# Post norms split by column halves, one factor pass moved by one unit, and score matmuls of two head groups interleaved, in a one-core decoder layer

## The chip, the cores and the metric

The kernel runs on one core of a Trainium2 chip. The metric is the device time of one execution in microseconds (us), lower is better. One profiled execution of the kernel gives the durations that are used below; three timed executions give the median that the change is compared with.

The engines are named as in the profile: PE is the matrix engine (its loading of the stationary operand is PEld), DVE the vector engine, ACT the scalar engine, POOL the GpSimd engine, and SP the engine whose queue issues nearly all DMAs here. [...]

## The reference

One layer is applied to a prompt of 1024 tokens and to 64 sample tokens (8 sequences of 8), all of width 1024, in float32. Post norms stand on the outputs, pre norms on the inputs:

```python
x = x + 0.5 * rms_norm(swiglu(rms_norm(x, norm_ffn1_pre), ffn1_w_gu, ffn1_w_down), norm_ffn1_post)
h = rms_norm(x, norm_mix_pre)
z = h @ w_in + b_in                      # q, k, v, hq, hf, hi, hg
a = attend(q, k, v, sinks)               # 8 heads of 64, 2 kv heads, window 128, sinks
o = hgrn2(silu(hq), f, hi, state)        # 4 heads of 128 x 128, gated recurrence
x = x + rms_norm(concat(rms_norm(a), rms_norm(o) * silu(hg)) @ w_out, norm_mix_post)
x = x + 0.5 * rms_norm(swiglu(rms_norm(x, norm_ffn2_pre), ffn2_w_gu, ffn2_w_down), norm_ffn2_post)

def rms_norm(x, g):
    return x * rsqrt(mean(x * x, axis=-1) + EPS) * g
```

The hidden width of each FFN is 2816. Outputs are both token groups, the last keys and values, and the recurrent states.

## The kernel before

**Token groups.** The 1088 tokens are cut into group 0 (two prompt blocks of 128 and the 64 samples, 320 columns) and groups 1 and 2 (three prompt blocks of 128 each). Group 0 is kept with features on the partitions all the way. Groups 1 and 2 come out of the down projections and out of `w_out` with tokens on the partitions, as two halves of 512 columns, `y[0]` and `y[1]`, each of shape 128 x 3 x 512: `y[hf][:, i]` is a piece of 128 tokens by 512 columns.

**Precision.** A weight or activation is split into a high and a low part (`split`, `load_w`, lines 251 to 263: a cast on ACT at L252 and a subtraction on DVE at L253), and every product is three matmuls (`mm3`, L273, L274, L275).

**FFN for groups 1 and 2.** The two groups are multiplied together by a seven-product scheme of the Strassen kind. In `f.up`, unit u (of 22) forms weight combinations on DVE (`factor`, `comb` at L662), seven products on PE, and evicts them (`evict`). After two units `left(u)` forms on POOL the combinations of the activations and stores them to DRAM (`FA`). The combinations of the down weights are formed in the same stage: `right_load(u)` loads four row pieces (L740), and `right_form(u)` computes four differences on POOL (L746 to L750) and stores them to DRAM (`FB`). Both are called in even units, at product 1 and at product 7. The down projections of groups 1 and 2 are then run product by product in `pair(ms)`: PA = (1, 6, 2), PB = (5, 3), PC = (7, 4). After PA, `y[0]` of group 1 is complete; after PB, `y[1]` of group 1; after product 7, `y[1]` of group 2; after product 4, `y[0]` of group 2 (`put`, L896 to L914).

**Streams.** Side work is written as generators. `stream(name, gen, rate)` registers one, `tick()` advances each by its rate after a piece of PE's main work, and `need(name)` emits what is left of it. The streams here: `m0`, `m1`, `m2` are the mixers (attention and recurrence) of the groups; `c0`, `c1`, `c2` are the norms between two stages for each group. The rate constants are `RA1` for the norms after FFN 1 and `RB1` for those after the mixer. The program order made this way is then re-ordered per engine by a scheduler that works on a simulated timeline, so that the place of an instruction in its queue is fixed at build time.

**Post norm of groups 1 and 2.** `post_n` (L411) loads both halves of the gain row, broadcast to 128 partitions (`bcast_row`, L396, scaled at L398), takes six sums of squares on ACT (`row_rms`, L388), the inverse root on DVE (L389, L390 and `rsqrt`), and then for each of six pieces (`post_block`) loads the residual piece `xt` (L405), multiplies by root and gain (L407, DVE), adds the residual (L408: half 0 on POOL, half 1 on DVE), and stores the result (L409). It is followed in the stream by the pre norm of the next stage: `pre_n` (before `w_in`) or `pre_s` (before FFN 2, with its own squares at L388, scaling at L435/L437 or L468/L470, and PE transposes at L445 or L488). `need("c1")` stands ahead of `w_in_units(1)`, and `need("c2")` ahead of `w_in_units(2)` and of FFN 2's `f2.up`.

**Output projection.** `w_out_units(n, ys)` for groups 1 and 2 runs, for each half, four weight pieces into three PSUM banks (of four of tag `mm`) and evicts them with three ACT copies (L1442).

**Attention.** `attn_block(n, b)` handles one block of 128 queries and 8 heads. It loops over the two kv groups g. For each g it makes two PSUM banks (`pr`), each with the scores of two heads (L1096). The heads of g = 0 lie on partitions 0 to 63 of the operands, those of g = 1 on partitions 64 to 127, so each score matmul contracts over 64 partitions. Then follow the masked row maximum on DVE (L1101), exponentials on ACT (L1110), transposes (L1121) and the products with v (L1134). The recurrence's steps are the PE matmuls at L1165 and L1189, which wait for DVE (L1200) and POOL (L1202).

## Time and profile before

| | |
|---|---|
| median of 3 timed executions | 2056.77 us (2053.96 to 2057.99) |
| the profiled execution's own time | 2056.1 us |
| its span, first to last instruction | 2054.4 us |
| mean granted PE clock | 0.989 |
| PE busy | 2017.0 us (98%) |
| DVE busy | 1453.1 us (71%) |
| ACT busy | 930.8 us (45%) |
| POOL busy | 572.4 us (28%) |

The profiled execution lies 1.7 us above its span and 0.7 us below the median. Read the table as follows: PE is the engine that is nearly always at work, so time can be saved in two ways only, by less time of PE's own work or by fewer stretches in which PE waits or runs at a lower granted clock. The other engines matter where PE waits for them.

| stage (PE) | about, us from the span's start |
|---|---|
| FFN 1: up and down, product set PA | 0 to 660 |
| w_in of group 0 | 660 to 735 |
| PB and PC, with the mixer of group 0 beside them | 735 to 870 |
| w_in and w_out stages, FFN 2's first units for group 0 | 870 to 1470 |
| FFN 2: up | 1470 to 1805 |
| FFN 2: down, all product sets | 1805 to 2046 |

### The profile page before, as it was taken

The numbers are of one execution on the slowest core, as the hardware profiler recorded it, in microseconds if no ns is written. First come the engines' busy times: TensorE is split into PE (matmuls) and PEld (weight loads), VectorE is DVE, ScalarE is ACT, GpSimd is POOL, SyncE is SP. The second block draws the span as 40 slices with busy tenths as digits, with TensorE's granted clock in tenths as the row PEclk, the third lists the DMA queues.
The fourth block names the chain that finished last, engine by engine and source line by source line (L and its number), as shares of the span: only waits on it lengthen the run. The fifth ranks groups of instructions, "written<-read, shape, count | busy, mean of one in ns | idle before, by whom it ended". The sixth has DMA issues, their size and how long they took to land.

```text
span 2054.4 us, 34787 instructions
## 1 busy us (share of the span) xinstructions
PE 2017.0 (98%) x13337; PEld 1884.0 (92%) x13337; DVE 1453.1 (71%) x2414; ACT 930.8 (45%) x1661; POOL 572.4 (28%) x523
## 2 busy tenths in 40 slices
PE   9999999999999999899999999899999999999998
PEld 8999999999988988798899898798899999999886
DVE  6775657886568556876668755775888888755657
ACT  6544333444454345344344433655544444444453
POOL 0033334554114001312212301311145555410202
PEclk9999999999999999899999999999999999999999
DMA  8545345556777546555344343535665556576874
GB/s 254 158 157 167 119 162 187 189 181 205 239 236 211 154 144 185 151 161 163 109 104 133 91 133 94 160 102 168 197 209 188 175 194 208 181 239 220 291 253 140
DMA packets 371976, 360.09 MB, mean 175 GB/s; under 512 B 40195, under 2 KB 293970, under 8 KB 371794
## 3 DMA queue, kind: packets, MB, share of 16 engines
q1 hardware_dynamic: 371009, 356.42, 55.3%
q8 instruction: 105, 1.72, 0.4%
q10 hardware_dynamic: 800, 1.44, 0.2%
q14 instruction: 62, 0.50, 0.1%
HBM read 279.85 MB, written 78.94 MB: 175 GB/s over the span
## 4 chain that ended last, share of the span: by engine, by line
PE 90%; DVE 5%; DMA 2%; issue 1%; ACT 1%; SPq 0%; POOL 0%; DVEq 0%; ACTq 0%
PE mm L273 26%; PE mm L274 26%; PE mm L275 26%; PE pv L1134 1%; PE sc L1096 1%; PE c L273 1%; PE c L275 1%; PE c L274 1%; DMA raw<-in_ffn_w_gu_dram 1%; PE lv L1165 1%; DVE wspl L253 1%; DVE w L253 1%; PE pT L1121 1%; DVE big L407 1%; DVE t L662 1%
## 5 line engine op out<-in xcount | busy, mean ns | idle before, releaser
L273 PE MATMUL mm<-h,wsph 128*128 128x320 f32 (+1 forms) x1296 | 411.7, 321 | 6.9 <-ACT sg L623 4.5
L274 PE MATMUL mm<-h,wsph 128*128 128x320 f32 (+1 forms) x1296 | 412.8, 319 | 0.0
L275 PE MATMUL mm<-h,wspl 128*128 128x320 f32 (+1 forms) x1296 | 410.6, 318 | 1.2 <-DVE sm L321 1.0
L253 DVE TENSOR_TENSOR wspl<-raw,wsph 128x1024 fp32r<-128x1024 f32 x202 | 257.8, 1278 | 125.6 <-ACT wsph L252 125.2
L252 ACT CAST wsph<-raw 128x1024 fp32r<-128x1024 f32 x202 | 211.2, 1048 | 293.1 <-PE mm L274 221.3
L253 DVE TENSOR_TENSOR w<-raw,w 128x512 fp32r<-128x512 f32 (+1 forms) x226 | 233.6, 1036 | 93.3 <-ACT w L252 89.4
L252 ACT CAST w<-raw 128x512 fp32r<-128x512 f32 (+1 forms) x226 | 169.7, 754 | 220.1 <-PE mm L274 110.1
L273 PEld LDWEIGHTS mm<-h,wsph 128*128 128x128 f32 x1296 | 245.0, 190 | 10.4 <-ACT sg L623 5.2
L274 PEld LDWEIGHTS mm<-h,wsph 128*128 128x128 f32 x1296 | 245.5, 189 | 3.4 <-issue 2.7
L275 PEld LDWEIGHTS mm<-h,wspl 128*128 128x128 f32 x1296 | 245.1, 189 | 2.8 <-DVE sm L321 1.2
L273 PE MATMUL mm<-h,w 128*128 128x384 f32 x704 | 236.6, 336 | 0.4 <-DVE big L716 0.4
L274 PE MATMUL mm<-h,w 128*128 128x384 f32 x704 | 236.3, 336 | 0.0
L275 PE MATMUL mm<-h,w 128*128 128x384 f32 x704 | 231.1, 336 | 0.7 <-DVE w L253 0.7
L700 POOL TENSOR_TENSOR big<-big 128x384 f32<-128x384 f32 x88 | 106.3, 1208 | 318.8 <-ACT big L713 235.0
L253 DVE TENSOR_TENSOR w<-t,w 128x512 fp32r<-128x512 f32 x176 | 177.7, 1019 | 21.5 <-ACT w L252 21.5
L274 PE MATMUL mm<-w,h 128*128 128x512 f32 x462 | 181.2, 392 | 0.0
L273 PE MATMUL mm<-big,w 128*128 128x384 f32 x528 | 176.6, 334 | 4.1 <-ACT w L252 4.1
L275 PE MATMUL mm<-w,h 128*128 128x512 f32 x462 | 180.1, 392 | 0.0
L273 PE MATMUL mm<-w,h 128*128 128x512 f32 x462 | 179.3, 392 | 0.0
L274 PE MATMUL mm<-big,w 128*128 128x384 f32 x528 | 176.5, 334 | 0.0
L275 PE MATMUL mm<-big,w 128*128 128x384 f32 x528 | 176.2, 334 | 0.0
L273 PEld LDWEIGHTS mm<-h,w 128*128 128x128 f32 x704 | 132.6, 188 | 1.1 <-DVE big L716 0.8
(344 smaller groups left out, 3929.7 us busy)
## 6 DMA issues: line engine op xcount, KB each, us to landing
raw<-in_ffn_w_gu_dram SPq DMA_DIRECT2D x156, 512.0 KB
raw<-in_ffn_w_down_dram SPq DMA_DIRECT2D x74, 512.0 KB
raw<-in_w_in_dram SPq DMA_DIRECT2D x54, 512.0 KB
ar<-fa SPq DMA_DIRECT2D x70, 384.0 KB
big<-in_ffn_w_down_dram SPq DMA_DIRECT2D x88, 256.0 KB
fb<-big SPq DMA_DIRECT2D x44, 512.0 KB
raw<-fb SPq DMA_DIRECT2D x40, 512.0 KB
fa<-big SPq DMA_DIRECT2D x22, 768.0 KB
```

The lines of the kernel that those rows point to most:

```text
L252: S.copy(hi, src)
L253: (lo_eng or V).tensor_tensor(lo, src, hi.bitcast(F32), op=ALU.subtract)
L273: PE.matmul(out, a[0], b[0], start=first, stop=False, skip_group_check=resume)
L274: PE.matmul(out, a[0], b[1], start=False, stop=False, skip_group_check=resume)
L275: PE.matmul(out, a[1], b[0], start=False, stop=last, skip_group_check=resume)
L407: V.scalar_tensor_tensor(t, t, r, gb[hf], op0=ALU.mult, op1=ALU.mult)
L662: V.tensor_tensor(t, x, y, op=ALU.subtract)
L700: G.tensor_tensor(e[:, i], e[:, i], e[:, i + 1], op=ALU.mult)
L1096: PE.matmul(bank[:, i * 256:i * 256 + wk], zq[64 * g:64 * g + 64, 2 * pr + i, b * P:(b + 1) * P], kx[64 * g:64 * g + 64, k0:k0 + wk], star ...
L1121: PE.transpose(bank[:, (i * nk + kb) * P:(i * nk + kb + 1) * P], pt[pr][:, i, kb * P:(kb + 1) * P], ident)
L1134: PE.matmul(ob[:, hd * 64:hd * 64 + 64], pT[pr][:, (i * nk + kb) * P:(i * nk + kb + 1) * P], vn[:, vb, g * 64:g * 64 + 64], start=kb == 0, ...
L1165: PE.matmul(b4[cs, a, :32], x[:, a, cs], y[:, a, cs], start=True, stop=True)
```

## The change

There are five edits.

1. **Post norms by halves.** `bcast_row` becomes `gain_row` for one half. The new `half_n` takes the three squares of one half on ACT and multiplies its three pieces by the gain row on DVE; for FFN 1 it is started for a half as soon as that half is complete (`half1`). `post_n` then adds the sums, takes the root, and handles each piece with one DVE instruction: piece times root plus `xt`. All adds on POOL in `post_n` are gone.
2. **Mixer's post norm at eviction.** In `w_out_units` the ACT copy of each bank is replaced by an ACT square of the bank (with its sum) and a DVE multiplication of the bank by the gain row into `y`. The gain row is loaded per half, between the half's matmuls and its eviction.
3. **Order of the stages after PB.** PC = (7, 4) is run as two calls, (7,) and (4,), and the half of group 2 that product 7 completes is normed beside product 4. `RA1` goes from 0.6 to 0.75.
4. **Down factors in odd units.** `right_load` and `right_form` are called in odd units, for the same weight rows.
5. **Alternating score matmuls.** `attn_block` loops over `pr` outside and over g inside: the four score matmuls of a step go to two banks, one for each g, and alternate between partitions 0 to 63 and 64 to 127. The small per-head vectors are indexed accordingly.

```diff
-    def bcast_row(ap, scale):
...
+    def gain_row(ap, scale, hf):
+        g = tmp2("gb")
+        nc.sync.dma_start(g, ap[0:1, hf * 512:hf * 512 + 512].partition_broadcast(P))
+        if scale is not None:
+            V.tensor_scalar(g, g, scale, None, op0=ALU.mult)
         return g
...
-            V.scalar_tensor_tensor(t, t, r, gb[hf], op0=ALU.mult, op1=ALU.mult)
-            (V if hf else G).tensor_tensor(t, t, xt, op=ALU.add)
...
+    def half_n(y, hf, sm, gpost, scale):
+        for i in range(3):
+            S.activation(junk, y[hf][:, i], AF.Square, accum_out=sm[:, 0, 4 * hf + i:4 * hf + i + 1])
+        g = gain_row(gpost, scale, hf)
         yield
         for i in range(3):
+            V.tensor_tensor(y[hf][:, i], y[hf][:, i], g, op=ALU.mult)
+            yield
+
+    def post_n(n, y, sm, xsrc, xdst):
+        V.tensor_tensor(sm[:, 0, 0:3], sm[:, 0, 0:3], sm[:, 0, 4:7], op=ALU.add)
+        V.tensor_scalar(sm[:, 0, 0:3], sm[:, 0, 0:3], 1.0 / D, EPS, op0=ALU.mult, op1=ALU.add)
+        rsqrt(sm[:, 1, 0:3], sm[:, 0, 0:3], (sm[:, 2, 0:3], sm[:, 3, 0:3]))
+        for i in range(3):
+            for hf in range(2):
+                cs = slice(hf * 512, hf * 512 + 512)
+                xt = tmp2("xt")
+                nc.sync.dma_start(xt, xsrc[i * P:(i + 1) * P, cs])
+                t = y[hf][:, i]
+                V.scalar_tensor_tensor(t, t, sm[:, 1, i:i + 1], xt, op0=ALU.mult, op1=ALU.add)
+                nc.sync.dma_start(xdst[i * P:(i + 1) * P, cs], t)
             yield
...
         def right_load(u):
-            k = f.units[u][0]
+            k = f.units[u - 1][0]
...
-                    if m == 1 and u % 2 == 0:
+                    if m == 1 and u % 2:
                         right_load(u)
                     product(u, m)
                     evict(u, m)
-                    if m == 7 and u % 2 == 0:
+                    if m == 7 and u % 2:
                         right_form(u)
...
+            for pr in range(2):
+                pt, banks = [], [axbank("sc") for _ in range(2)]
+                for i in range(2):
+                    for g in range(2):
+                        PE.matmul(banks[g][:, i * 256:i * 256 + wk],
+                                  zq[64 * g:64 * g + 64, 2 * pr + i, b * P:(b + 1) * P],
+                                  kx[64 * g:64 * g + 64, k0:k0 + wk], start=True, stop=True)
...
+                g = gain_row(A["norm_mix_post"], None, hf)
                 for i in range(3):
-                    S.copy(y[hf][:, i], banks[i])
+                    S.activation(junk, banks[i], AF.Square, accum_out=sm[:, 0, 4 * hf + i:4 * hf + i + 1])
+                    V.tensor_tensor(y[hf][:, i], banks[i], g, op=ALU.mult)
...
-    RA0, RA1, RB0, RB1 = 1.2, 0.6, 0.6, 0.8
+    RA0, RA1, RB0, RB1 = 1.2, 0.75, 0.6, 0.8
...
-        f1.pair(PB, False, last=lambda: f1.begin_pair(PC, False))
+        half1(1)
+        f1.pair(PB, False, last=lambda: f1.begin_pair((7,), False))
         done1(1)
-        f1.pair(PC, False)
+        f1.pair((7,), False, last=lambda: f1.begin_pair((4,), False))
+        half1(2)
+        f1.pair((4,), False)
         done1(2)
...
-        stream("c1", post_n(1, f2.ys[1], x2N[0], A["norm_ffn2_post"], 0.5, O[0][0, t0:t0 + 384]), 1.5)
+        y, sm = f2.ys[1], small()
+        stream("c1", seq(*[half_n(y, hf, sm, A["norm_ffn2_post"], 0.5) for hf in range(2)],
+                         post_n(1, y, sm, x2N[0], O[0][0, t0:t0 + 384])), 1.5)
```

More of the change, by code (lines that the diff above doesn't have):

```diff
@@ L391, in row_rms @@
         rsqrt(sm[:, 1, b0:b1], sm[:, 0, b0:b1], (sm[:, 2, b0:b1], sm[:, 3, b0:b1]))
-    def bcast_row(ap, scale):
-        g = [tmp2("gb"), tmp2("gb")]
-        for hf in range(2):
-            nc.sync.dma_start(g[hf], ap[0:1, hf * 512:hf * 512 + 512].partition_broadcast(P))
-            if scale is not None:
-                V.tensor_scalar(g[hf], g[hf], scale, None, op0=ALU.mult)
-        return g
-    def post_block(n, y, i, r, gb, xsrc, xdst):
-        for hf in range(2):
-            cs = slice(hf * 512, hf * 512 + 512)
-            xt = tmp2("xt")
-            nc.sync.dma_start(xt, xsrc[i * P:(i + 1) * P, cs])
-            t = y[hf][:, i]
-            V.scalar_tensor_tensor(t, t, r, gb[hf], op0=ALU.mult, op1=ALU.mult)
-            (V if hf else G).tensor_tensor(t, t, xt, op=ALU.add)
-            nc.sync.dma_start(xdst[i * P:(i + 1) * P, cs], t)
@@ L411, in post_n @@
-    def post_n(n, y, xsrc, gpost, scale, xdst):
-        gb = bcast_row(gpost, scale)
-        sm = small()
-        row_rms(n, y, [0, 1, 2], sm)
+    def gain_row(ap, scale, hf):
[3 more added lines that the diff above has]
+            V.tensor_scalar(g, g, scale, None, op0=ALU.mult)
+        return g
+    def half_n(y, hf, sm, gpost, scale):
+        for i in range(3):
+            S.activation(junk, y[hf][:, i], AF.Square, accum_out=sm[:, 0, 4 * hf + i:4 * hf + i + 1])
+        g = gain_row(gpost, scale, hf)
@@ L416, in post_n @@
         yield
         for i in range(3):
-            post_block(n, y, i, sm[:, 1, i:i + 1], gb, xsrc, xdst)
+            V.tensor_tensor(y[hf][:, i], y[hf][:, i], g, op=ALU.mult)
[12 more added lines that the diff above has]
+                nc.sync.dma_start(xdst[i * P:(i + 1) * P, cs], t)
@@ L743, in right_form @@
         def right_form(u):
-            k = f.units[u][0]
+            k = f.units[u - 1][0]
             a, b = downs.pop(u)
@@ L1085, in attn_block, with of @@
             sm, mx = small(), small()
-            pts = {}
             ob = None
-            for g in range(2):
-                hs = slice(4 * g, 4 * g + 4)
-                pt = []
-                for pr in range(2):
-                    bank = axbank("sc")
+            def of(x, pr):
+                return x.rearrange("p (g r i) -> p g r i", g=2, r=2)[:, :, pr]
+            for pr in range(2):
[5 more added lines that the diff above has]
+                                  kx[64 * g:64 * g + 64, k0:k0 + wk], start=True, stop=True)
+                for g in range(2):
                     p = t2((P, 2, 256))
@@ L1095, in attn_block @@
                     for i in range(2):
-                        PE.matmul(bank[:, i * 256:i * 256 + wk],
-                                  zq[64 * g:64 * g + 64, 2 * pr + i, b * P:(b + 1) * P],
-                                  kx[64 * g:64 * g + 64, k0:k0 + wk], start=True, stop=True)
+                        hd = 4 * g + 2 * pr + i
+                        V.tensor_tensor_reduce(out=p[:, i, :wk], in0=banks[g][:, i * 256:i * 256 + wk], in1=mask,
+                                               op0=ALU.add, op1=ALU.max, scale=1.0, scalar=NEG,
+                                               accum_out=mx[:, 0, hd:hd + 1])
+                V.scalar_tensor_tensor(of(sm[:, 0], pr), of(mx[:, 0], pr), 0.125, of(sinkb, pr),
+                                       op0=ALU.mult, op1=ALU.max)
+                V.tensor_scalar(of(sm[:, 1], pr), of(sm[:, 0], pr), -1.0, None, op0=ALU.mult)
+                for g in range(2):
                     for i in range(2):
                         hd = 4 * g + 2 * pr + i
-                        V.tensor_tensor_reduce(out=p[:, i, :wk], in0=bank[:, i * 256:i * 256 + wk], in1=mask,
-                                               op0=ALU.add, op1=ALU.max, scale=1.0, scalar=NEG,
-                                               accum_out=mx[:, 0, hd:hd + 1])
-                V.scalar_tensor_tensor(sm[:, 0, hs], mx[:, 0, hs], 0.125, sinkb[:, hs],
-                                       op0=ALU.mult, op1=ALU.max)
-                V.tensor_scalar(sm[:, 1, hs], sm[:, 0, hs], -1.0, None, op0=ALU.mult)
-                for pr in range(2):
-                    for i in range(2):
-                        hd = 4 * g + 2 * pr + i
-                        S.activation(pt[pr][:, i, :wk], pt[pr][:, i, :wk], AF.Exp, bias=sm[:, 1, hd:hd + 1],
+                        S.activation(pt[g][:, i, :wk], pt[g][:, i, :wk], AF.Exp, bias=sm[:, 1, hd:hd + 1],
                                      scale=0.125, accum_out=mx[:, 1, hd:hd + 1])
-                V.tensor_tensor(sm[:, 2, hs], sinkb[:, hs], sm[:, 0, hs], op=ALU.subtract)
-                S.activation(sm[:, 2, hs], sm[:, 2, hs], AF.Exp)
+                V.tensor_tensor(of(sm[:, 2], pr), of(sinkb, pr), of(sm[:, 0], pr), op=ALU.subtract)
+                S.activation(of(sm[:, 2], pr), of(sm[:, 2], pr), AF.Exp)
                 yield
@@ L1116, in attn_block @@
                 pT = []
-                for pr in range(2):
+                for g in range(2):
                     bank = axbank("pT")
@@ L1121, in attn_block @@
                             PE.transpose(bank[:, (i * nk + kb) * P:(i * nk + kb + 1) * P],
-                                         pt[pr][:, i, kb * P:(kb + 1) * P], ident)
+                                         pt[g][:, i, kb * P:(kb + 1) * P], ident)
                     t = t2()
@@ L1128, in attn_block @@
                     ob = axbank("pv")
-                for pr in range(2):
+                for g in range(2):
                     for i in range(2):
@@ L1134, in attn_block @@
                             PE.matmul(ob[:, hd * 64:hd * 64 + 64],
-                                      pT[pr][:, (i * nk + kb) * P:(i * nk + kb + 1) * P],
+                                      pT[g][:, (i * nk + kb) * P:(i * nk + kb + 1) * P],
                                       vn[:, vb, g * 64:g * 64 + 64], start=kb == 0, stop=kb == nk - 1)
@@ L1416, in mixer, with w_out_units @@
                 nc.sync.dma_start(O[4][0, 0].rearrange("h k v -> k h v"), state[0])
-        def w_out_units(n, ys):
+        def w_out_units(n, ys, sums):
             w = WIDTH[n]
@@ L1431, in w_out_units @@
             y = ys[n] = [big(F32, (P, 3, 512)), big(F32, (P, 3, 512))]
+            sm = sums[n] = small()
             for hf in range(2):
@@ L1475, in misc @@
                               A[src][0, :, 8:128].rearrange("b w g d -> b w (g d)"))
+    sums = {}
     def done1(n):
@@ L1481, in done1, with half1 @@
         else:
-            stream(f"c{n}", seq(post_n(n, y, xN[n - 1], A["norm_ffn1_post"], 0.5, x1N[n - 1]),
-                                pre_n(n, y, g, hmix)), RA1)
+            need("half")
+            stream(f"c{n}", seq(half_n(y, 2 - n, sums[n], A["norm_ffn1_post"], 0.5),
+                                post_n(n, y, sums[n], xN[n - 1], x1N[n - 1]), pre_n(n, y, g, hmix)), RA1)
+    def half1(n):
+        sums[n] = small()
+        stream("half", half_n(f1.ys[n], n - 1, sums[n], A["norm_ffn1_post"], 0.5), RA1)
     with tc.tile_pool(name="f1", bufs=1) as tp:
@@ L1508, in done_mix @@
         else:
-            stream(f"c{n}", seq(post_n(n, y, x1N[n - 1], A["norm_mix_post"], None, x2N[n - 1]),
+            stream(f"c{n}", seq(post_n(n, y, sums[n], x1N[n - 1], x2N[n - 1]),
                                 pre_s(n, y, g, part, f2.SF)), RB1)
@@ L1524, in tile_step @@
         stream("m1", mixer(1), RM[1])
-        w_out_units(0, ym)
+        w_out_units(0, ym, sums)
         done_mix(0)
@@ L1532, in tile_step @@
         stream("m2", mixer(2), RM[2])
-        w_out_units(1, ym)
+        w_out_units(1, ym, sums)
         done_mix(1)
@@ L1537, in tile_step @@
         need("m2")
-        w_out_units(2, ym)
+        w_out_units(2, ym, sums)
         done_mix(2)
@@ L1559, in ready_half @@
         y = f2.ys[2][1]
-        gb = tail["gb"] = bcast_row(A["norm_ffn2_post"], 0.5)
+        gb = tail["gb"] = [gain_row(A["norm_ffn2_post"], 0.5, hf) for hf in range(2)]
         sm = tail["sm"] = small()
```

## Prediction

> **What bounds the kernel now.** I read the page's busy shares first, then its line of granted PE clock. PE works nearly all the time:

> ```profile
> span 2054.4 us, 34787 instructions
> PE 2017.0 (98%) x13337; PEld 1884.0 (92%) x13337; DVE 1453.1 (71%) x2414; ACT 930.8 (45%) x1661; POOL 572.4 (28%) x523
> ...
> PEclk9999999999999999899999999999999999999999
> ```

> So two things can save time: less PE work, or fewer waits of PE. The timeline of PE, which gives in brackets the idle time before a row and its releaser, puts the waits of the middle stages in three places (two rows of each of the first two):

> ```profile
> 852.77 0.66 PE L1165 MATMUL lv<-t,t 128*32 128x32 f32 x32 [3.43 <-DVE t L1200]
> 862.03 1.09 PE L1071 MATMUL oT<-ident,t 128*128 128x128 f32 x4 [2.09 <-DVE t L1067]
> ...
> 1288.66 0.47 PE L273 MATMUL mm<-h,wsph 128*128 128x320 f32 x1 [2.34 <-ACT sg L623]
> 1306.00 0.66 PE L1165 MATMUL lv<-t,t 128*32 128x32 f32 x32 [3.25 <-DVE t L1200]
> ```

> With their smaller neighbours, place B (838 to 863) has 7.8 us of idle PE, place C (1283 to 1310) 7.3, and place D (1430 to 1513, FFN 2's first units) 6.6, of which 4.1 is one wait at 1481.79. After them the granted clock falls. Windows of 10 us (length, then busy us of PE, PEld, DVE, ACT, POOL, then clock, DMA share, GB/s) show that, and that DVE is full beforehand:

> ```profile
> 840.00:850.00 10.00, 7.96 (x97) 5.78 (x95) 9.09 (x36) 7.82 (x22) 3.02 (x3) 1.00 0.98 272
> 850.00:860.00 10.00, 6.18 (x72) 5.71 (x72) 7.67 (x18) 3.88 (x9) 2.69 (x6) 0.60 0.67 149
> 860.00:870.00 10.00, 7.97 (x44) 7.56 (x45) 7.57 (x18) 3.52 (x7) 0.62 (x1) 0.72 0.19 52
> ...
> 1475.00:1485.00 10.00, 6.79 (x43) 6.47 (x41) 10.00 (x10) 1.62 (x3) 7.88 (x4) 1.00 0.40 149
> ```

> PE's busy time times the missing share of clock is 6.18 x 0.40 + 7.97 x 0.28 = 4.7 us at B; in the same way 3.9 at C (0.83 and 0.66) and 1.5 at D (0.83). So B, C and D cost 21.7 of idle and 10.1 of slow clock, 31.8 us. DVE is full there with post norms, as DVE's timeline of group 2's mixer norm shows; POOL's rows lie beside it:

> ```profile
> 1426.88 6.16 DVE L407 SCALAR_TENSOR_TENSOR big<-big,sm,gb 128x512 f32<-128x512 f32 x6
> 1432.97 1.78 DVE L408 TENSOR_TENSOR big<-big,xt 128x512 f32<-128x512 f32 x1
> ...
> 1439.09 0.68 DVE L408 TENSOR_TENSOR big<-big,xt 128x512 f32<-128x512 f32 x1
> ```
> ```profile
> 1427.72 1.74 POOL L408 TENSOR_TENSOR big<-big,xt 128x512 f32<-128x512 f32 x1 [39.25 <-DVE big L407]
> ```

> The same add takes 0.68 us alone and 1.78 beside a POOL add; L407 takes 0.74 and up to 1.79. From the first L407 to the end of the last add it is 12.9 us.

> **The score matmuls.** One float32 matmul is two records. PE's timeline shows what one pair of scores of the same head group costs (1.06 to the next row's start), two such pairs in a row (1.92), and, at L1368, one matmul of 32 partitions (1.05) and two that stand on different partitions and banks (1.06):

> ```profile
> 1123.60 1.13 PE L1096 MATMUL sc<-kx,big 64*128 64x256 f32 x4
> 1124.66 0.44 PE L273 MATMUL mm<-h,wsph 128*128 128x384 f32 x1
> ...
> 1009.72 1.99 PE L1096 MATMUL sc<-kx,big 64*128 64x256 f32 x8
> 1011.64 0.42 PE L273 MATMUL mm<-h,wsph 128*128 128x320 f32 x1
> ...
> 979.00 1.12 PE L1368 MATMUL su<-t,t 32*128 32x512 f32 x2
> 980.05 0.87 PE L1362 MATMUL sav<-big,t 128*64 128x128 f32 x6
> ...
> 955.41 1.13 PE L1368 MATMUL su<-t,t 32*128 32x512 f32 x4
> 956.47 0.50 PE L273 MATMUL mm<-wsph,h 128*128 128x512 f32 x1
> ```

> So two neighbours on separate partitions run at the price of one. The built order of the changed kernel has 16 steps of four score matmuls. In 9 the two groups alternate; in 6 the scheduler has still put one bank's pair, other work, then the other's: nothing changes there. In one the pairs stand next to each other without alternating: 2.12 - 1.92 = 0.2 saved. Of the 9, five stood as eight records before and go from 1.92 to 1.06 (0.86 each, 4.3); two stood apart and go from 2.12 to 1.06 (2.1); two are the half-sized ones of the first block (0.9, 1.09 to about 0.64). Together 7.5 us. Bounds: 0.4 if 64-partition pairs do not overlap (only adjacency is won), 7.5 if they do; I take the upper end, since L1368 differs only in 32 for 64 partitions, less 1.0 for the step ahead of B, where PE soon waits anyway: 6.5.

> [...]

> **Post norms.** Behind the root, six DVE instructions remain, spaced 0.66 where POOL is quiet: 4.0 us instead of 12.0 at B (833.10 to 845.08), 11.4 at C, 12.9 at D. Six gain multiplications of about 0.68 move ahead of the root: for FFN 1's first half beside the preceding products, for the mixer into the eviction. Fifteen POOL adds (1.3 to 1.75 each) go; DVE gets 15 instructions more, 10 us in all, against some 10 us of slowed L407 and L408. The chains at B and C still wait for xt (one landing is 4.03 in the chain at 840), and much of PE's idle is the recurrence's own step (L1200) in DVE's queue. So I take neither all nor nothing of the 31.8 but a third: 10.6 (bounds 0 and 31.8). The squares, 0.73 with their read each, only move on ACT, which is 45% busy. In the tail the norm of group 1 (1999 to 2020) ends 25 us before PE does; the closing 9.1 us behind PE's last matmul are the same code. Price 0 while PE's products cover it; without cover, three multiplications, 2.0.

> **Eviction.** ACT's copy (0.58) becomes square and multiplication, 0.82 + 0.68, and the multiplication waits for the gain row. What queues behind: on DVE the next weight splits and scan steps, on PE the second bank of the next half, since only one of four banks is free. In the built order the first gain row stands on SP behind three weight loads. After the half's last matmul the last of these needs a split (1.05 ACT, 1.21 DVE), then the row lands (xt, same size: 4.03), then 0.68: 7.0 us. PE's cover, also by the built order, is 24 matmuls on the free bank (0.231 each, 5.5) plus scans, values and scores (about 2.7). The other three evictions are alike, with 6 to 9 us of cover. Between 0 and 4 each; I take 1.5 in all, as cover and wait are nearly equal.

> **The rest.** In the build, ACT loads its function table two times fewer; one is the 1.28 us load at 993.16, inside a PE wait of 2.37 that ACT ends: -1.3 (bounds 0 and 1.3). The down factors: four DMAs of 256 KB, two stores and four POOL instructions move by one unit (14.5 us). In FFN 1 PE never waits there, price 0, hidden by PE's 50.0 of 50 us; at FFN 2's start POOL's two sets (1472 to 1483, 1494 to 1501) slow DVE splits from 0.68 to 1.78; the second leaves the crowd. This is part of D's third; at most 2 lost if the factors collide with `left`. Splitting PC reloads nothing; its prefetch starts in the same place: 0, at most one landing of 4. RA1 only starts steps earlier.

> **Sum**, against the profiled execution's own 2056.1 (0.7 below the median): 2056.1 - 6.5 - 10.6 - 1.3 + 1.5 = 2039.2. I forecast 2039. Less than 0.2% (4 us) can't be told from no change here.

> **Rivals.**
> - *Waits only move*: DVE's backlog at B, C and D comes from splits and scans, so the stalls stay. For it: the releasers are L1200, not L408. Against: 6.6 + 2.4 us of DVE at B are post norm. Scores and eviction alone: 2056.1 - 6.5 + 1.5 = 2051. Chance 0.20, split 0.12 faster and 0.08 same.
> - *Row pairs don't overlap*: 2056.1 - 0.4 - 10.6 - 1.3 + 1.5 = 2045. Only the 64 partitions speak for it. Chance 0.10.
> - *Full clock comes back*: if halved gaps no longer lower the clock, all 10.1 is saved beside a third of 21.7 (7.2): 17.3 instead of 10.6, 2032.5. Against: the 2.34 gap at 1286 is followed by 0.83. Chance 0.14. [...]
> - *Slower: the gain row is late.* If a weight load (4.95 in the chain at 1486) must land in front of it, each of four evictions holds PE for 7.0 + 4.95 - 5.5 = 6.45, 25.8 in all, and the norm gains, behind the same eviction, are lost: 2056.1 - 6.5 + 25.8 = 2075. It decides from 1.6 us per eviction if nothing else is won, from 4.6 if the other terms hold. Against: the covers above. Chance 0.11.

> My forecast has 0.45. **Range:** from 2028 (three fifths of the 31.8, 19.1, all 7.5 of the scores, the 1.3, and no price at eviction: 2056.1 - 27.9) to 2056 (the terms eaten up by evictions at 4 each); above it lies the slower rival at its price, below it a full recovery. Faster: 0.45 + 0.14 + 0.10 + 0.12 = 0.81; same 0.08; slower 0.11.

> **What would show it.** The score steps that alternate should take 1.06 instead of 1.92. L407's successor should take 0.74 each with POOL idle beside it, and the chain from root to last add about 4 to 6 us. B, C and D should hold about 21 us of idle and slow clock. The forecast is wrong if new PE waits stand ahead of the second bank after `w_out` evictions, or if PE's waits for L1200 keep their length.

## The result and the profile after

The changed kernel takes 2035.4 us (median of 4 runs, 2034.9 to 2035.9) against 2056.4 of the kernel before (median of 4, 2054.0 to 2058.0). The ratio is 0.9899, 95% interval 0.9882 to 0.9916: about 21 us less. The forecast was 2039, in a range from 2028 to 2056. So the time came out right; its terms did not all do so, and the experiments show which.

The page of the profiled execution, whose span is 20.8 us shorter:

```profile
span 2033.6 us, 34788 instructions
...
PE 2002.3 (98%) x13337; PEld 1870.8 (92%) x13337; DVE 1445.4 (71%) x2429; ACT 921.4 (45%) x1647; POOL 550.4 (27%) x508
...
PEclk9999999999999999899999999999999999999999
```

PE's busy time fell by 14.7 us with the same 13337 matmuls. Part of that is the scores, which overlap; part is clock, since a matmul at a lowered clock counts as a longer busy time (in `e10`, one of 128x384 takes 0.33 us at clock 1.00 and 0.52 at 0.50).

**Where the time went**, by events that stand in both traces, mostly matmuls of the recurrence, since other work changes places (start before minus start after): 0.6 us are won up to the end of place B (869), 7.8 by 1050, 10.5 by 1266, 19.1 by 1338, 17.6 by 1392 (so something is given back), 18.8 by 1486 and 20.8 at the end.

**Place B** kept its waits. PE's timeline, with the idle time ahead of a row and its releaser in brackets:

```profile
843.25 0.46 PE L1171 MATMUL lv<-t,t 128*32 128x32 f32 x32 [1.24 <-DVE sm L1144]
...
855.23 1.08 PE L1195 MATMUL l<-t,t 128*64 128x64 f32 x8 [3.22 <-DVE t L1206]
859.78 1.09 PE L1075 MATMUL oT<-ident,t 128*128 128x128 f32 x4 [3.46 <-DVE t L1071]
```

With the smaller ones it is 9.8 us of idle, 7.8 before. And DVE's timeline shows why the shorter norm did nothing here (the first, third and fourth of the six instructions that follow the root are shown):

```profile
824.05 0.74 DVE L421 SCALAR_TENSOR_TENSOR big<-big,sm,xt 128x512 f32<-128x512 f32 x1
...
840.69 0.75 DVE L421 SCALAR_TENSOR_TENSOR big<-big,sm,xt 128x512 f32<-128x512 f32 x1 [4.24 <-DMA xt<-in_x_prompt_dram]
841.82 0.75 DVE L421 SCALAR_TENSOR_TENSOR big<-big,sm,xt 128x512 f32<-128x512 f32 x1 [0.38 <-DMA xt<-in_x_prompt_dram]
```

Five of the six take 0.74 or 0.75, as forecast (the last 1.14), but from the first to the end of the last it is 22.1 us (824.05 to 846.11) and not 4. Two things stand in between. DVE's queue holds other work there, among it the gain multiplications of the second half (826.95, 3.64 us for the three), which the second of the six needs. And the residual `xt` comes late: DVE sits idle for it 4.24 and 0.38, since SP issues that load only at 835.20, behind the store of the second piece and three weight loads. The last add before ended at 845.1, so this norm ends no earlier. Where both are there in time, group 2's mixer norm, the six take 5.2 us (1411.2 to 1416.4; 12.9 before).

B's last wait even grew, from 2.09 to 3.46: at 855.01 DVE weights group 2's first half (1.88 us), ahead of the recurrence's step and of the attention's root, behind which L1075 waits. The runs below with FFN 1's early halves all have 3.46 or more there, the three without FFN 1's new norm 2.08 or 2.09.

**A place of which the prediction had counted only a table load**, call it E: PE's wait of 2.37 at 996 before. Windows of 10 us of before (length, busy us of PE, PEld, DVE, ACT, POOL, then clock, DMA share, GB/s), and below them one of after:

```profile
990.00:1000.00 10.00, 7.63 (x37) 6.03 (x37) 6.20 (x11) 4.27 (x5) 1.69 (x2) 0.77 0.55 160
1000.00:1010.00 10.00, 10.00 (x89) 8.38 (x88) 5.16 (x17) 1.74 (x10) 4.03 (x8) 0.89 0.19 55
```
```profile
990.00:1000.00 10.00, 10.00 (x95) 9.32 (x93) 8.26 (x19) 4.92 (x6) 2.01 (x3) 1.00 0.61 170
```

E cost 2.37 of idle and 7.63 x 0.23 + 10 x 0.11 = 2.9 of slow clock, 5.2 us; after, PE is full there and at full clock.

**Place C and the evictions.** PE's waits between 1250 and 1400 (us in total, times, longest), then windows of C's first half, of `w_out` of group 2 (1385) and of D (1470):

```profile
PE mm L273 <- DVE big L1451: 3.9, 2, 3.1
PE mm L273 <- ACT h L1062: 1.4, 1, 1.4
```
```profile
1265.00:1275.00 10.00, 8.21 (x37) 8.21 (x38) 6.93 (x32) 3.98 (x11) 0.00 (x0) 0.66 0.17 52
```
```profile
1385.00:1395.00 10.00, 8.57 (x35) 6.45 (x36) 4.85 (x6) 4.27 (x6) 0.00 (x0) 1.00 0.68 198
...
1470.00:1480.00 10.00, 8.78 (x50) 8.26 (x49) 9.94 (x12) 3.98 (x9) 4.63 (x3) 1.00 0.66 223
```

The waits of before at 1283 to 1310 (for `sg` and for the step L1200) are gone. In their place PE waits 3.09 us for L1451, the eviction's multiplication, at 1263.7, and the clock after it falls to 0.66, another 8.21 x 0.34 = 2.8. The shorter waits around 1385 (0.66, 1.43 and 0.84) leave the clock at 1.00. Place D (1470 to 1510) holds 2.1 us of idle at full clock, 8.1 of both before.

What moved at C is the root. DVE's timeline, of before and then of after, shows the root's first step and, after, the first of the six instructions behind it:

```profile
1292.40 0.16 DVE L389 TENSOR_TENSOR sm<-sm 128x3 f32<-128x3 f32 x1 [2.56 <-ACT junk L388]
```
```profile
1260.20 0.16 DVE L412 TENSOR_TENSOR sm<-sm 128x3 f32<-128x3 f32 x1 [0.41 <-ACT junk L1450]
...
1280.70 0.75 DVE L421 SCALAR_TENSOR_TENSOR big<-big,sm,xt 128x512 f32<-128x512 f32 x1 [1.82 <-DMA xt<-x1N]
```

Before, the last copy of group 1's `w_out` ends at 1263.1, and the root waits for the squares until 1292.4. With the squares in the eviction it starts at 1260.2, right behind the last of them. The six instructions then take 10.0 us (1280.70 to 1290.67; 11.4 before), not 4, and they start late again for the residual: SP issues its loads at 1275.97, behind a weight load that waits 11.4 us for a split (L253). An earlier load of the residual was not tried.

**A score step** of both groups, all four matmuls in eight records, to the next row's start:

```profile
1021.04 1.14 PE L1099 MATMUL sc<-kx,big 64*128 64x256 f32 x8
1022.11 0.41 PE L273 MATMUL mm<-h,wsph 128*128 128x320 f32 x1
```

### The profile page after: what moved, and what is told of

It is laid out like the page before. It is cut to its first block, busy times and chain, and to the rows that moved or that the text cites. A ratio compares the mean times of both kernels' runs of the same rounds, so it can differ in the third digit from the quotient of the medians.

```text
span 2033.6 us, 34788 instructions
## 1 busy us (share of the span) xinstructions
PE 2002.3 (98%) x13337; PEld 1870.8 (92%) x13337; DVE 1445.4 (71%) x2429; ACT 921.4 (45%) x1647; POOL 550.4 (27%) x508
## 4 chain that ended last, share of the span: by engine, by line
PE 94%; DVE 3%; DMA 2%; issue 1%; ACT 0%; DVEq 0%; SPq 0%; ACTq 0%
PE mm L273 27%; PE mm L274 27%; PE mm L275 27%; PE pv L1140 1%; PE c L275 1%; PE c L273 1%; PE c L274 1%; DMA raw<-in_ffn_w_gu_dram 1%; PE sc L1099 1%; PE lv L1171 1%; PE pT L1127 1%; PE tr L492 1%; DMA xt<-x1N 0%; PE l L1195 0%; PE sav L1368 0%
## 5 line engine op out<-in xcount | busy, mean ns | idle before, releaser
L273 PE MATMUL mm<-h,wsph 128*128 128x320 f32 (+1 forms) x1296 | 413.5, 321 | 3.5 <-DVE big L1451 3.1
L253 DVE TENSOR_TENSOR wspl<-raw,wsph 128x1024 fp32r<-128x1024 f32 x202 | 251.8, 1249 | 112.4 <-ACT wsph L252 112.0
L253 DVE TENSOR_TENSOR w<-raw,w 128x512 fp32r<-128x512 f32 (+1 forms) x226 | 248.0, 1101 | 92.1 <-ACT w L252 90.3
L273 PEld LDWEIGHTS mm<-h,wsph 128*128 128x128 f32 x1296 | 244.7, 189 | 8.3 <-DVE big L1451 3.5
L273 PE MATMUL mm<-h,w 128*128 128x384 f32 x704 | 235.6, 335 | 0.8 <-DVE big L720 0.8
L273 PE MATMUL mm<-w,h 128*128 128x512 f32 x462 | 180.2, 393 | 0.0
L704 POOL TENSOR_TENSOR big<-big 128x384 f32<-128x384 f32 x88 | 111.8, 1271 | 240.1 <-ACT big L717 121.2
L273 PE MATMUL mm<-big,w 128*128 128x384 f32 x528 | 176.6, 334 | 0.0
L253 DVE TENSOR_TENSOR w<-t,w 128x512 fp32r<-128x512 f32 x176 | 161.0, 924 | 17.5 <-ACT w L252 17.3
L273 PEld LDWEIGHTS mm<-h,w 128*128 128x128 f32 x704 | 132.1, 188 | 1.3 <-DVE big L720 1.2
```

Of the source, the lines that this page charges most:

```text
L253: (lo_eng or V).tensor_tensor(lo, src, hi.bitcast(F32), op=ALU.subtract)
L273: PE.matmul(out, a[0], b[0], start=first, stop=False, skip_group_check=resume)
L704: G.tensor_tensor(e[:, i], e[:, i], e[:, i + 1], op=ALU.mult)
```

## The experiments

Times are medians of 4 to 11 runs; "won" is the fall against the kernel before, run on the same chip, as the ratio's distance from 1 times 2055. Every ratio carries 0.1 to 0.17% on either side (2 to 3.5 us), and the difference of two ratios some 4.5 us, so differences of one or two microseconds between kernels are not read, and the text says where two intervals overlap. The traced execution is not always near the median: that of `e8` lies 3.9 us below it, that of `e1` 2.8 below, that of `e10` 3.7 above.

**Each part alone, on the kernel before**

*Scores alone* (`e1_scores_only`): before, with the changed kernel's loop over `pr`, `i`, `g` in `attn_block`.

> The kernel before with one part of the change: the score matmuls of the two head groups alternate. Theory (terms add): the score steps' own time falls by 7 to 8 us as in the changed kernel (34.4 to 26 us), a little of it in places where PE waits anyway, so 2056.4 becomes 2049 to 2051. Rival (waits only move): PE waits for DVE at B and C whatever it does earlier, and half of the saving ends there: 2052 to 2054. Rival (order): the scheduler's new order, not the scores, gave the 21 us; then this part alone gives a number outside both, below 2045 or above 2055.

Measured: 2051.9, ratio 0.9985 (0.9975 to 0.9994), 3.1 won. The theory's 5 to 7 was too much. PE is busy with the score matmuls for 27.7 us instead of 32.6 (the 34.4 of the expectation also counts a wait of 3.25 inside a step), a fall of 4.9 only: the list scheduler alternated seven of the 16 steps here, nine in the changed kernel. PE's waits at B for the recurrence's step (L1200 before, one line of the same text here) grew from 4.2 to 5.5. So both the rival of moving waits and a smaller gain in work have a share.

*Down factors alone* (`e3_down_only`):

```
-            k = f.units[u][0]
+            k = f.units[u - 1][0]
-                    if m == 1 and u % 2 == 0:
+                    if m == 1 and u % 2:
```

> The kernel before with the down factors alone moved to odd units. Theory: no gain of its own in FFN 1, where PE never waits there, and at most part of what place D gave: 2055 to 2057, that is no change. Rival (the factors were what filled DVE's and POOL's time at D): D's 2 to 2.5 us come from here, 2054. Rival (they collide with another load in the odd units): 2058 or more, with new idle of PE every second unit of FFN 1.

Measured: 2050.7, ratio 0.9978 (0.9968 to 0.9987), 4.5 won. My theory fell; this is the rival, and larger than it said. 3.7 of the trace's 5.4 us come between 1392 and 1486, at D, where PE's wait of 4.1 us is gone. DVE's timeline at D, of before and then of this kernel, shows the same two steps, 1.78 us each before and 0.68 here:

```profile
1478.43 1.78 DVE L253 TENSOR_TENSOR w<-raw,w 128x512 fp32r<-128x512 f32 x1
1480.13 1.78 DVE L662 TENSOR_TENSOR t<-raw,raw 128x512 f32<-128x512 f32 x1
```
```profile
1476.74 0.68 DVE L253 TENSOR_TENSOR w<-raw,w 128x512 fp32r<-128x512 f32 x1
1477.34 0.68 DVE L662 TENSOR_TENSOR t<-raw,raw 128x512 f32<-128x512 f32 x1
```

Before, POOL's four instructions of `right_form` run from 1472.6 to 1483.0, beside the weight splits that FFN 2's second unit waits for. Moved by one unit they begin at 1479.7, when these splits are done. The four splits that follow then take 5.77 us beside them instead of 2.48 (1482.46; 1486.78 before), but PE waits no more than 0.5 at a time behind those.

*The mixer's norm alone* (`e8_mixer_only`): before, with squares and weighting in `w_out_units`, and the new `post_n` behind it (and in the tail).

> The kernel before with the mixer's post norm alone changed: squares and weighting at w_out's eviction, one instruction per piece behind the root (and the same single instruction in the closing norms, whose cover stays). FFN 1's norms, scores and down factors as before. Theory (this part carries what scores, 3, and factors, 4.5, leave of the 21): places C and D lose 8 to 13 us, 2055 becomes 2043 to 2047, the norm's last add at C comes 15 us or more earlier. Rival (parts only work together, as the sum of single parts falls short): 2050 to 2054, with C's waits for the running state's step as long as before.

Measured: 2050.1, ratio 0.9968 (0.9956 to 0.9980), 6.6 won; in the profiled execution 9.9. The median lies in the rival's range and short of the theory's 8 to 13, but the place is the theory's: in the trace C gives 8.0 (2.2 won at 1266, 10.2 at 1338), and `w_out` of group 2 gives 1.4 back. The last piece of C's norm is done at 1298.6 instead of 1309.9: 11 us, less than the 15 expected. Of PE's waits at C these are left, and none for the step:

```profile
PE mm L273 <- DVE big L1477: 3.0, 2, 2.2
PE mm L273 <- ACT h L1090: 1.4, 1, 1.4
```

So the eviction's wait belongs to this part and to no other.

*FFN 1's early halves alone* (`e9_ffn1_halves`): before, with `half1`, the new `done1`, PC split and RA1 0.75.

> The kernel before with the early halves of FFN 1 alone: groups 1 and 2 square and weight the first half ahead of the second, one instruction per piece behind the root, PC split, RA1 0.75. The mixer's norms, scores and factors as before. Theory (the early half is worth as much alone as leaving it out cost in the changed kernel, about 10): 2044 to 2047, with the waits at B and the wait of 2.37 at 996 shorter. Rival (the early half only repairs what weighting by a row of its own costs, so that place B ends as it was, and the gain is the 3 us of the table load and of the stretch behind B): 2051 to 2054.

Measured: 2048.8, ratio 0.9974 (0.9964 to 0.9985), 5.3 won; in between the two. The trace, of the fastest of its eight runs, says where: -0.5 up to 869, +5.0 at 1052, and 3.7 more between 1266 and 1338. B is as it was, as the rival said; the gain ahead of 1052 is place E:

```profile
990.00:1000.00 10.00, 10.00 (x93) 9.70 (x91) 8.27 (x19) 3.97 (x4) 2.88 (x6) 1.00 0.55 157
```

It is group 2's norm of FFN 1 that came earlier: its last add ended at 940.6 before, its last instruction ends at 927.5 here. Behind it ACT's and PE's rows stand in another order, and neither the wait at 996 nor its slow clock returns. The earlier end is not the reason, though: in the two runs without early halves below this norm ends at 958.0 and 943.3, and the wait is gone all the same. What all runs without the wait share is FFN 1's new norm, and 23 loads of ACT's function table instead of 25; the two are not separated.

**One part taken out of the changed kernel**

*Without the alternating scores* (`e2_no_scores`): the old loop over `g`, then `pr`.

> The changed kernel without the alternating scores: each group's two score matmuls stand together as before. Theory (terms add): 2035.4 + 6 to 8 = 2041.5 to 2043.5, and the score steps take 34 us again. Rival (waits only move): the rest of the change gave nearly all, 2036 to 2039. Rival (the scores are most of it): above 2048.

Measured: 2042.1, ratio 0.9937 (0.9923 to 0.9950). Against the changed kernel's 0.9899 the scores are worth 0.38%, 7.8 us, as the theory said; the score matmuls are busy for 31.8 us instead of 24.0, and PE as a whole 7.2 us longer (2009.5).

*Down factors back in even units* (`e10_no_down`).

> The changed kernel with the down factors back in even units. Theory (their gain adds to the others): 2035.4 + 3.5 to 5 = 2039 to 2040.5, with PE's wait of some 4 us for a weight split at the first units of FFN 2 back. Rival (the mixer's norm already relieves place D, the factors do nothing more): 2034.5 to 2036.5.

Measured: 2038.5, ratio 0.9917 (0.9904 to 0.9931): 0.18%, 3.7 us worse, with overlapping intervals, so a loss is likely and not shown. The size is the theory's, the place only in part; the trace is of the slowest of the five runs. At D, PE waits 1.3 for `w` behind ACT (4.1 in the kernel before), and 2.3 us less are won there than in the changed kernel (from 1392 to 1575). Another 3.9 less are won between 870 and 1050, where the traces differ in a slow clock from 938 to 945 (last section). A slow clock comes there in `e11` too (939.89 to 943.30), whose factors are in odd units.

*Eviction by copies* (`e4_copy_evict`):

```
-                g = gain_row(A["norm_mix_post"], None, hf)
-                    S.activation(junk, banks[i], AF.Square, accum_out=...)
-                    V.tensor_tensor(y[hf][:, i], banks[i], g, op=ALU.mult)
+                    S.copy(y[hf][:, i], banks[i])
...
+  seq(*[half_n(y, hf, sums[n], A["norm_mix_post"], None) for hf in range(2)], post_n(...), pre_s(...))
```

> The changed kernel with the eviction of w_out put back: ACT copies the three banks, and the mixer norm takes its squares and its six gain multiplications afterwards, ahead of the root, as the halves of FFN 1 do; one instruction per piece stays behind the root. Theory A (the late gain row costs what PE waits for L1451 show, 4.3 us, and the multiplications are as cheap later): 2031 to 2033, with no wait of PE on the banks' eviction. Theory B (weighting at eviction is what shortens the wait at C, since six multiplications of 0.68 stand in DVE's queue between the half and the root): the waits at C and D come back by 4 to 8 us, 2036 to 2040, although the eviction's waits go.

Measured: 2050.4, ratio 0.9972 (0.9963 to 0.9980), 15 us worse than the changed kernel; theory A fell, B was right in kind and half in size. The eviction's waits went, and much more came: the squares follow the copies, so the root's first step waits for them until 1282.87 (1260.20 in the changed kernel); six multiplications of 0.68 stand in DVE's queue between 1277.9 and 1288.8, the root's steps are mixed with them and end after 1291, and the residual lands later still (DVE's timeline):

```profile
1303.71 0.75 DVE L421 SCALAR_TENSOR_TENSOR big<-big,sm,xt 128x512 f32<-128x512 f32 x1 [3.27 <-DMA xt<-x1N]
...
1310.02 0.75 DVE L421 SCALAR_TENSOR_TENSOR big<-big,sm,xt 128x512 f32<-128x512 f32 x1 [1.90 <-DMA xt<-x1N]
```

The norm ends at 1315.7 instead of 1290.7, and so `w_out` of group 2 and D follow late: what was won up to 1338 (16.4) is 5.9 at 1392 and 4.8 at 1575. The run moves squares and multiplications together, so it does not say which of the two costs more.

*Early halves taken out* (`e5_no_early_half`): both halves go through `half_n` in `done1`, PC in one call, RA1 0.6; and (`e12_late_halves`) the same with PC split and RA1 0.75 kept.

> The changed kernel without the early halves of FFN 1: both halves of groups 1 and 2 are squared and weighted only when both are complete, PC is one pair of pieces again, and RA1 is 0.6. Weighting in the mixer's eviction, the single instruction behind the root, down factors and scores stay. Theory (the mixer's weighting at eviction carries the gain of the norms, the early halves little, since place B kept its 9.8 us of idle): 2035 to 2038. Rival (the norms of FFN 1 end earlier by the six multiplications and everything behind B profits): 2041 to 2046, with B's idle 3 us or more longer.

> The changed kernel with FFN 1's halves squared and weighted only when both are complete, but PC split and RA1 0.75 as in the changed kernel. It tells whether the 10.7 us that leaving out the early halves, the split and the rate cost together came from the halves. Theory (the halves): 2043 to 2047, with waits at B and for the cache's key load behind it. Rival (the split and the rate): 2035 to 2038.

Measured: 2046.1, ratio 0.9954 (0.9942 to 0.9966), 11 us worse than the changed kernel, and 2041.9, ratio 0.9941 (0.9928 to 0.9953), 8.6 worse. My theory for the first fell, the rival holds; the second lies just below what the halves alone were to give, so most of it is the halves; the intervals of the two overlap, and what the split and the rate add is not shown. B's waits of the first of the two (PE, 820 to 890):

```profile
PE skT L1288 <- DMA kv<-in_cache_k_win_dram: 5.6, 2, 4.6
PE l L1195 <- DVE t L1206: 4.1, 1, 4.1
```

Group 1's norm ends at 867.6 instead of 846.1, and the load of the cache's keys, on the same SP queue as the norm's residuals and stores, has become a wait of its own.

**Three attempts at a better version**

*Gain row ahead of the half's weights* (`e6_gain_early`), *all score steps chained to alternate* (`e7_all_alternate`, each matmul issued after the one before it), and *both, the row ahead of the last weight piece* (`e11_alternate_gain`):

```
             for hf in range(2):
+                g = gain_row(A["norm_mix_post"], None, hf)   # e6; in e11 inside the kk loop, at kk == 3
                 banks = [mmbank() for _ in range(3)]
...
-                    for g in range(2):
-                        PE.matmul(...)
+                    for g in (1, 0):
+                        with tc.issue_after(before):         # e7 and e11; not for a step's first
+                            before = PE.matmul(...).ins
```

> The changed kernel with the gain row of each half of w_out requested ahead of that half's weights instead of behind them. Theory (the eviction's waits are the gain row, as forecast): PE's waits for L1451, 4.3 us, go, and 2031 to 2033 results. Rival (the eviction waits for DVE's own queue and ACT's squares, not for the row): the waits for L1451 stay above 3 us, 2034 to 2037. Rival (the order written out changes more than the row): below 2029 or above 2038.

> The changed kernel with all 16 score steps chained so that the groups alternate after the step's first matmul (in six of them other work still stands behind that first one). Theory (overlap is PE work saved wherever it stands): six or seven steps save one matmul of 0.5 us each, 3 us, 2032 to 2033. Rival (the chain delays scores whose second bank comes free late, and DVE's softmax with them): 2036 to 2040.

> The changed kernel with all score steps chained to alternate, as in the run with that change alone (2034.4), and the gain row requested ahead of the last of the half's four weight pieces, between the two places tried. Theory (half of the eviction's waits were the row's place; the earliest place was worse because it moved weights and DVE's order): 2031 to 2033, PE's waits for L1451's successor under 2 us. Rival (any other place reorders DVE's queue and costs elsewhere what it saves): 2035 to 2040.

Measured: 2040.2 (0.9923, 0.9911 to 0.9936), 2034.4 (0.9895, 0.9883 to 0.9908) and 2036.3 (0.9911, 0.9898 to 0.9925). In the first the waits for L1451 did fall, but DVE's new order put others in their place (PE's waits between 1220 and 1400), and one of 3.6 for L720 at 1496.6 besides:

```profile
PE mm L273 <- ACT sg L627: 1.9, 2, 1.0
PE mm L273 <- DVE big L1451: 1.8, 2, 1.0
...
PE hT L1226 <- DVE t L1222: 1.4, 1, 1.4
```

In the second the score matmuls' busy time fell by another 2.6 us (24.0 to 21.4) and PE's busy time by 4.4, while the wait ahead of L1075 at B grew from 3.46 to 5.92 and one of 2.46 came up at 847.8: the time is that of the changed kernel within its interval. The third kept a wait of 3.0 for the eviction. None reached the 2031 to 2033 of the theories, and none beats the changed kernel measurably.

## Why the prediction came out right, step by step

**The parts add up, alone.** 3.1 + 4.5 + 6.6 + 5.3 = 19.5 us won by single parts, each 2 to 2.5 us either way, against 20.8 by all. Taken out one at a time they cost 7.8 + 3.7 + 15 + 11.3 = 37.8. Most of the difference lies in the norms: `e4` and `e5` do not go back to the old norm, they keep the new one without its early squares and weighting, and that is worse than the old: the squares and six multiplications of all rows stand ahead of the pieces without cover. Worked out from the single parts, the old mixer norm beside the other three would give an estimate of 2055 - 12.9 = 2042; `e4` has 2050. "One instruction behind the root" pays only together with "squares and weighting at eviction".

**Scores, -6.5: right in mechanism, and between the two measured sizes.** The alternating steps take 1.06, as forecast. The step whose pairs only stand next to each other, priced at 0.2, overlaps as well: 4.23 with 3.09 of idle in it, so 1.14 instead of 2.12. Alone the scores won 3.1, taken out they cost 7.8, and PE's busy time in them fell by 8.5. The 1.0 taken off for the step ahead of B is borne out: alone, B's waits for the recurrence's step grew by 1.3. The rival "row pairs don't overlap" is out.

**Post norms, -10.6 of 31.8 at B, C and D: too small in sum, and wrong in place and in mechanism.** Without the eviction's own waits B, C and D hold 14.6, so 17.2 are gone and not 10.6: 0.2 at B, 11.0 at C, 6.0 at D. At B 9.8 of idle and 2.5 of slow clock are 12.3, where there were 12.5. The step that failed is "4.0 us instead of 12.0 at B", and the same at C: the six instructions take 22.1 and 10.0, since the residual's late load, and at B the second half's multiplications, keep them apart. The sentence that the chains at B and C still wait for `xt` had it, and the rival "waits only move" fits B. What won at C was a term put at nothing: the squares do not "only move on ACT", in the eviction they let the root start at 1260.2 instead of 1292.4. No run takes squares and weighting apart, so their shares are open. "B, C and D hold about 21" was 14.6 without the eviction and 20.5 with it.

**D was ascribed to the wrong part.** The prediction saw that POOL's sets slow DVE's splits from 0.68 to 1.78 at 1472 to 1483, but gave the factors no term of their own ("part of D's third"). Moved alone, they win 4.5.

**The table load, -1.3: a term mis-sized for its place.** The load was one part of E; with the rest of the wait and the slow clock behind it E was 5.2, all gone. It goes with FFN 1's new norm (`e9`): `e1`, `e3` and `e8`, which keep the old one, keep the wait at 996 and all 25 table loads.

**Eviction, +1.5: too small by 5.7 us.** One of the four evictions had a wait of 3.09 and with it 2.8 of slow clock, two others 0.42 and 0.84: 7.2 us, near half of the 16 of the bounds. The slow clock behind a wait was not in the price. What is known of the cause: with the row early the waits shrink from 4.3 to 1.8, so the row's place (and DVE's order planned by it) is more than half of it. In the largest wait DVE is busy with its queue right up to the multiplication at 1266.05; only at 1388.97 does DVE itself sit idle for the row, 2.71. The waits of 0.66 and 1.43 around 1385 come with the mixer's norm as well (`e8` has both) and were in no term.

**Why 2039 was near 2035: in part luck.** In the two traces the terms come to 8.5 (scores) + 17.2 (B, C and D) + 5.2 (E) - 7.2 (eviction) - 2.1 (the waits beside it) = 21.6, where the span fell by 20.8. The forecast had 6.5 + 10.6 + 1.3 - 1.5 = 16.9. Three gains were larger than forecast and the eviction was dearer, and these errors largely cancel. The prediction's own signs of being wrong, new waits behind `w_out` evictions and waits for the recurrence's step that keep their length, both came true (3.09 at C; 4.1 at B, 4.2 before), and the time was right all the same. Two smaller slips: evictions at 4 each eat up 16 of 18.4, which gives 2054 and not the range's 2056, and POOL's adds took up to 1.97, not 1.75.

**The tail, price 0: right.** From PE's last matmul to the end it is 9.03 us, 9.11 before.

**"Full clock comes back" was the wrong question.** That rival, and the reason against it, let the clock depend on the length of a wait. The runs show no such length: between 820 and 1520 the slow clock lasted 34.1 us before (ten times 3.41) and 17.1 in the changed kernel (five times), but of waits of about the same length 2.09 (`e7`) had no such 3.41 us behind it, 2.24 (`e8`) one and 2.37 (E) two (last section).

**Open.** How much of `e10`'s and `e1`'s few microseconds is the part itself, and how much the other order and the slow clock, can't be told apart here: every edit moves what comes after it.

## What to carry to other kernels

When a chain behind a root is shortened, look at the next input it needs: at B six instructions of 0.74 spread over 22 us, behind a late residual and late multiplications; they closed up to 5.2 us only where both were early. Look also at what the root itself waits for: at C that was the larger part. Moving work ahead of a reduction pays only where it really stands ahead, in the producer's own eviction: the same squares and multiplications put behind the copies cost more than the old form. And price a wait of TensorE with the slow clock behind it: here that took about as much as the wait, 2.9 us beside 2.37 at E and 2.8 beside 3.09 at the eviction.

## What the runs showed of the hardware

**The slow clock came in stretches of whole multiples of 3.41 us.** Windows of 1 us around the eviction of the changed kernel, and around 938 in the run with the factors in even units (clock is the third number from the end):

```profile
1265.00:1266.00 1.00, 0.00 (x0) 0.00 (x0) 1.00 (x5) 0.00 (x0) 0.00 (x0) 1.00 0.90 270
1266.00:1267.00 1.00, 0.21 (x1) 0.21 (x2) 1.00 (x3) 0.00 (x0) 0.00 (x0) 0.50 0.80 240
...
1272.00:1273.00 1.00, 1.00 (x6) 1.00 (x6) 0.00 (x0) 0.00 (x0) 0.00 (x0) 0.58 0.00 0
1273.00:1274.00 1.00, 1.00 (x9) 1.00 (x8) 0.00 (x0) 0.82 (x1) 0.00 (x0) 1.00 0.00 0
```
```profile
938.00:939.00 1.00, 1.00 (x5) 0.33 (x4) 0.93 (x4) 0.00 (x0) 0.00 (x0) 0.60 0.00 0
...
944.00:945.00 1.00, 1.00 (x5) 1.00 (x4) 0.83 (x1) 0.00 (x0) 0.00 (x0) 0.50 0.71 209
945.00:946.00 1.00, 1.00 (x12) 0.54 (x12) 0.00 (x0) 0.00 (x0) 0.00 (x0) 0.99 0.00 0
```

So a wait had no fixed price here. 2.24 us in the run with the mixer's norm alone were followed by one stretch of 3.4 us, 2.37 at E by one of 6.8, 2.09 at 1293 in the run with all steps alternating by none; and the 6.8 us at 938 follow a wait of 0.58 and then 2.1 us of light matmuls (128x64, 8x64 and 32x512), which without the wait (changed kernel, 936 to 939) left the clock at 1.00. Nor did each stretch follow a wait. In the third attempt (`e11`) PE is busy without a gap from 925 to 945 (1.00 in each window of 1 us), and a slow stretch still starts at 939.89:

```profile
937.00:938.00 1.00, 1.00 (x10) 0.59 (x10) 0.93 (x6) 0.00 (x0) 0.00 (x0) 1.00 0.00 0
...
940.00:941.00 1.00, 1.00 (x4) 1.00 (x5) 1.00 (x3) 1.00 (x2) 0.00 (x0) 0.50 0.58 152
```

What decides whether a wait or light work has a slow stretch behind it, these runs do not show. With PE full, 3.41 us at 0.50 cost half of their length; that is an estimate from these figures, 1.7 us. Why the runs of one kernel spread over several microseconds (2050.9 to 2059.4 before) was not tested.

**Four score matmuls, two on each half of the partitions, took the time of two.** Where they are neighbours in the queue in the order A, B, A, B, their eight records take 1.07 us (1021.04 to 1022.11); before, the four records of two matmuls of one group take 1.06 (1123.60 to 1124.66) and the eight of two such pairs 1.92 (1009.72 to 1011.64). The one step that stands as A, A, B, B in the built order takes 1.14 (1262.56), and in the trace's records the matmuls of both kinds start in pairs, 0.007 us apart in the first and 0.013 in the second.
